# A two-layer encoder trunk: half of each row normalized from the sum just made on chip, x loaded two steps ahead, and the weight scalings moved into the output pass

## The chip, the cores and the metric

The kernel runs on one core of a Trainium2 chip. The metric is the device time of one execution in microseconds (us), the smaller the better. A change of 0.2% is about 5.5 us here.

## The reference

A sequence of 2048 rows of width 1024 goes through two layers. Cut to what matters:

```python
# layer A: gated MLP with a spatial mix in groups of 128 rows
h = rms_norm(x, a_norm_g)
u, v, z = split(h @ w_in, 3)                 # each 2048 x 2048
v = layer_norm(gelu(v), ln_g, ln_b)
y = gelu(u) * (w_s @ v + b_s) * silu(z)      # w_s masked by chunks of 64, per head
x = x + y @ w_out                            # 2048 x 2048 times 2048 x 1024
# layer B: attention over a band of 9 chunks of 64 rows
k, v = split(rms_norm(x, kv_norm_g) @ w_kv, 2)
q, z = split(rms_norm(x, b_norm_g) @ w_qz, 2)
o = softmax(q k^T / 8 + rel_bias) v
x = x + (o * silu(z)) @ w_out_b
return rms_norm(x, final_norm_g)
```

All is in float32. The kernel makes a float32 product out of three TensorE matmuls (high by high, high by low, low by high), after a split of each operand: ScalarE (ACT) casts the high half, VectorE (DVE) subtracts it for the low half.

## The kernel before, in words

**Products.** Layer A and the V projection are computed with Strassen's scheme in Winograd's form: a product of 2x2 block matrices in seven block products. The seven are called phases and are run in the order `PH = (1, 2, 6, 5, 7, 4, 3)`. In each phase an index j runs over 0 to 7, a pair of row blocks of 128 rows: block 2j is the upper half of the matrix (r = 0), block 2j+1 the lower (r = 1). One phase and one j make a step. A step of the passes in front (named n = 0 to 5: n = 0, 1 make v, n = 2 to 5 make u and z together, in quarters) has 12 matmuls of 512 columns, a step of the output pass ("o", y @ w_out) has 24, a step of the V pass ("v", x1 @ w_v) has 12. Tiles are P for n = 0 to 5, Po and Pv for the last two.

**Which phase finishes what.** A result block (r, c), c the half of the columns, is finished in phase 2 for (0,0), phase 7 for (1,1), phase 4 for (1,0) and phase 3 for (0,1); `evict` (L349) then adds the PSUM tile to a running sum in SBUF and calls `done_out` (L833) for the output pass. There x is added to it and the sum, x1 = x + y @ w_out, is stored to DRAM as `x1d`. So a row block 2j+1 is complete in step (phase 4, j), and 2j in step (phase 3, j).

**Order of the work.** `run_steps` emits, step by step, first the events of the step, then the matmuls, then the split of the left operand for three steps later (`LOOK = 3`), then the loads and splits of weights. `later(k, f)` puts f some steps on. The framework schedules from this, and each engine runs its own list strictly in order; so does SP, whose queue issues all DMAs: an issue that waits for a sum or a free buffer holds all issues behind it.

**Output pass, left operand.** Phase by phase, `prep_out` (L804) loads y blocks into tiles A (`y_load`, 4 buffers) and splits them into So. `s2_of` (L797) makes `sc` from three of them in steps 0 to 7. In phase 3 `prep_out` loads one block more and subtracts `sc` from it on VectorE (L822), three steps ahead of the product.

**Adding x.** For (0,0), (1,1) and (1,0) `done_out` loads x into a tile xr in the very step of the product (L851) and adds it one step later (L843): on VectorE for r = 0, on GpSimd (POOL) for r = 1. For (0,1), `x_ahead` (L854) loads x in phase 4 and adds it to the running sum on GpSimd (L857) before phase 3 has been added.

**Rows for V.** When the four pieces are in DRAM, `row_load` (L928) loads a block's two halves back into tiles bx, at the steps nin+43+j (odd blocks) and nin+51+j (even blocks), nin being the first step of the output pass; it has 56 steps, so most even blocks come in the V pass. Two steps on, `row_norm` (L936) squares both halves on ScalarE (jn, L941), adds the two sums on VectorE (L945, tile rn), raises to -1/2 on GpSimd (L946), and scales both halves on ScalarE (bx, L950). Four steps on, `row_flip` (L954) has TensorE transpose the eight 128x128 tiles into tn (L960), ScalarE copies them (L962), and they are stored as `xTd` for the V pass and the layer behind it. A transpose stands in TensorE's list between the matmuls of two steps, so what it waits for, those matmuls wait for too.

**Scalings.** Eleven weight blocks (eight of w_v, three of the first K, Q, Z projection) are multiplied by the norm gains on GpSimd and stored back (`scaled`, L878: a load of 512 KB into a `raw` tile, a multiply two steps on, a store four steps on). Before them come eight jobs (`o_sums`, `o_last`) that make the combinations of w_out. All nineteen sit at the places of the list `spare` (L913), before the start of phases 5, 7, 4, 3 of n = 2 and 1, 5, 7, 4, 3 of n = 3, 4, 5. The four `raw` buffers are shared with the loads of every pass's weights (rw, rwo, rwv). Sums and x tiles share the 25 buffers of the tag `acc`.

Of the kernel before, what the change touches and what calls it, by code (L numbers as in the profile page):

```python
# [12 lines left out]
AF = mybir.ActivationFunctionType  # L13
ALU = mybir.AluOpType
# [3 lines left out]
P = 128  # L18
# [9 lines left out]
EPS = 1e-6  # L28
# [5 lines left out]
def trunk_kernel(  # L34
# [19 lines left out]
    nc = tc.nc  # L54
# [4 lines left out]
    x1d = [dram.tile([T, D], F32, name=f"x1d{t}") for t in range(NT)]  # L59
# [24 lines left out]
    mhalf = cst.tile([P, 1], F32, name="mhalf")  # L84
# [116 lines left out]
    with ExitStack() as actx:  # L201
# [144 lines left out]
        xa = {}  # L346
        ya = {}
# [56 lines left out]
        def later(steps, f_):  # L404
            late.append((now[0] + steps, f_))
# [262 lines left out]
        start = {}  # L668
# [5 lines left out]
        def at(s, f_):  # L674
            events.setdefault(s, []).append(f_)

        for n in range(6):
            for ph in PH:
# [4 lines left out]
                elif n > 2:  # L683
                    o = -13 if ph == 6 else -5
# [103 lines left out]
        sc = {}  # L788

        def y_load(r, c, j, ph):  # L790
            t = pos[0].tile([P, 2, 512], F32, tag="A", name=f"A{ph}_{r}{c}_{j}", bufs=4)
            nc.sync.dma_start(t[:], ytd[r, c, j][:])
            return t[:]

        tv, tg = nc.vector.tensor_tensor, nc.gpsimd.tensor_tensor

        def s2_of(j):  # L797
# [3 lines left out]
                pieces(a[:, g], a[:, g], b[:, g], add)  # L801
            tv(sc[j], a, sc[j], op=sub)

        def prep_out(ph, j):  # L804
            if ph == 1:
                v = sc[j] = pos[0].tile([P, 2, 512], F32, tag="sc", name=f"sc{j}", bufs=8)[:]
                nc.sync.dma_start(v, ytd[0, 0, j][:])
            elif ph == 2:
                v = y_load(0, 1, j, ph)
            elif ph == 6:  # L810
                v = sc[j]
            elif ph == 5:
                v, b = y_load(1, 0, j, ph), y_load(1, 1, j, ph)
                tv(v, v, b, op=add)
            elif ph == 7:
                v, b = y_load(0, 0, j, ph), y_load(1, 0, j, ph)
                tv(v, v, b, op=sub)
            elif ph == 4:
                v = y_load(1, 1, j, ph)
            else:  # L820
                v, a = sc[j], y_load(0, 1, j, ph)
                tv(v, a, v, op=sub)  # L822
            views = []
            for g in range(2):
                t = s_tile(f"So{ph}_{j}_{g}")
                split(
                    t[:, 0].rearrange("p a b -> p (a b)"),
                    t[:, 1].rearrange("p a b -> p (a b)"), v[:, g, :], "So",
                )
                views += s_views(t)  # L830
            return views

        def done_out(n, r, c, j, t):  # L833
            blk = 2 * j + r
            cs = slice(c * 512, c * 512 + 512)
            rs = slice(blk % TB * P, (blk % TB + 1) * P)

            def store():
                nc.sync.dma_start(x1d[blk // TB][rs, cs], t)

            if (r, c) != (0, 1):
                xr = x_rows(r, c, j)
                later(1, lambda: (tg if r else tv)(t, t, xr, op=add))  # L843
                later(2, store)
            else:
                later(1, store)

        def x_rows(r, c, j):
            blk = 2 * j + r
            xr = acc_tile(f"xr{blk}_{c}")  # L850
            nc.sync.dma_start(xr[:], x[blk * P : (blk + 1) * P, c * 512 : c * 512 + 512])  # L851
            return xr[:]

        def x_ahead(r, c, j):  # L854
            xr = x_rows(r, c, j)
            s_ = (xa if r else ya)["o", j][:]
            later(2, lambda: tg(s_, s_, xr, op=add))  # L857

        def act_out(s, ph, j, views):
            flush(s)  # L860
# [4 lines left out]
        nin = start["o", 1]  # L865
# [8 lines left out]
            add_t(ts, start["o", ph], "o", ph, rows_o, 4, where, None, offs)  # L874
        for j in range(NJ):
            at(nin + j, lambda j=j: s2_of(j))
            at(start["o", 4] + j + 1, lambda j=j: x_ahead(0, 1, j))
        def scaled(src, name, gain, keep):  # L878
            raw = sh.tile([P, 1024], F32, tag="raw", name=f"raw_{name}", bufs=4)
            nc.sync.dma_start(raw[:], src)  # L880
            k = gain.shape[1]
            r3 = raw[:].rearrange("p (k c) -> p k c", k=k)
            later(2, lambda: nc.gpsimd.tensor_tensor(
                r3, r3, gain.broadcast_to([P, k, 1024 // k]), op=mul
            ))
            later(4, lambda: nc.sync.dma_start(keep, raw[:]))

        jobs = [
            (w_vv[r, c, q], f"bv{r}{c}{q}", kg[:, 4 * r + 2 * q : 4 * r + 2 * q + 2, :],
# [20 lines left out]
            later(2, lambda: tg(a, a, c[:], op=sub))  # L910
            later(4, lambda: nc.sync.dma_start(wos[4, q][:], a))

        spare = [(n, ph) for n in (2, 3, 4, 5) for ph in (1, 5, 7, 4, 3)][1:]  # L913
        todo = [lambda q=q, f_=f_: f_(q) for q in range(4) for f_ in (o_sums, o_last)]
        todo += [lambda job=job: scaled(*job) for job in jobs]
        for at_, f_ in zip(spare, todo):
            at(start[at_] - 3, f_)

        nxp = []
        xn = {}  # L920
# [6 lines left out]

        def row_load(blk):  # L928
            t, b = divmod(blk, TB)
            xn[blk] = [acc_tile(f"bx{blk}_{c}") for c in range(2)]  # L930
            for c, xt in enumerate(xn[blk]):
                nc.sync.dma_start(
                    xt[:], x1d[t][b * P : (b + 1) * P, c * 512 : c * 512 + 512]
                )

        def row_norm(blk):  # L936
            xs = xn[blk]
            jk = nxp[0].tile([P, 2, 512], BF16, tag="xv", name=f"jn{blk}", bufs=4)
            rs = [sm.tile([P, 1], F32, tag="rr", name=f"rn{blk}_{c}", bufs=6) for c in range(2)]
            for c in range(2):  # L940
                nc.scalar.activation(  # L941
                    jk[:, c, :], xs[c][:], AF.Square, scale=1.0 / 32, accum_out=rs[c][:],
                )
            r = rs[0]
            nc.vector.tensor_scalar(r[:], r[:], rs[1][:], EPS, op0=add, op1=add)  # L945
            nc.gpsimd.tensor_tensor(r[:], r[:], mhalf[:], op=ALU.pow)  # L946

            def scale():
                for xt in xs:
                    nc.scalar.mul(xt[:], xt[:], r[:])  # L950

            later(2, scale)

# [91 lines left out]
        for ph in PH:  # L1045
            if ph == 1:
                where, offs = in_big("v", ph, ("hh",)), ((-5, 1), (-4, 1), (-3, 1))
            else:
                where = in_t("v", ph)
                o = -12 if ph == 6 else -6  # L1050
# [3 lines left out]
                chain_in("v", "hl"), offs,  # L1054
            )
        for j in range(NJ):
            for blk, s_ in ((2 * j + 1, nin + 43 + j), (2 * j, nin + 51 + j)):
                ts.setdefault(s_, []).append(lambda blk=blk: row_load(blk))
                at(s_ + 2, lambda blk=blk: row_norm(blk))
                at(s_ + 4, lambda blk=blk: row_flip(blk))  # L1060
            at(nv + 2 + 9 * j // 8, lambda j=j: s7_of_v(j))
            at(start["v", 6] + 2 + j, lambda j=j: s4_of_v(j))
# [474 lines left out]
```

## Time and profile before

| what | value |
|---|---|
| three runs | 2740.37, 2740.96, 2745.56 us; median 2740.96 |
| the profiled execution | 2740.26 us |
| its span, first to last instruction | 2738.5 us |
| TensorE (PE) busy | 2648.9 us, 97% |
| VectorE, ScalarE, GpSimd busy | 1964.3, 1317.9, 781.7 us |
| granted TensorE clock, mean | 0.989 |
| output pass, first to last matmul, about | 1067 to 1387 us |
| V pass, about | 1388 to 1560 us |

The profile counts an engine as busy while an instruction of its own runs; matmuls overlap, so the time that TensorE loses is read from its waits and from the rows of equal windows. In a row of the waits stand the waiting engine, the tile and line, what it waited for, and the total, the count and the longest in us. In a row of windows stand the window, its length, the busy time of PE, the weight loads, DVE, ACT and POOL with their counts, the granted clock, the share of the DMA engines and GB/s. In a row of the timeline stand the start, the duration, the engine (SPq is SP's DMA queue), line, operation, out<-in, and in brackets the idle time before it and what ended that. Groups end in: busy us, mean ns of one | idle before, and its releasers.

### The profile page before, as it was taken

To read this page: it belongs to the slowest core of one execution; us is meant where nothing else is said; L and a number is where in the kernel's file an instruction comes from. 1 tells how busy PE (TensorE), PEld (TensorE's weight loads), DVE (VectorE), ACT (ScalarE), POOL (GpSimd) and SP (SyncE) were. 2 spreads that over 40 slices of the span, in tenths; PEclk is the share of its full clock that TensorE was granted. 3 is DMA by queue.
4 is the path that set the end of the run, shared out by engine and by line. 5 is a ranking of instruction groups with operands and counts; after the bars stand their busy time and mean duration, and the time that the engine had idled before them with its cause. 6 is when DMAs were issued, how large, how long until landed. Compare 5 with 4: busy or idle time off the path is not lost. (4 is left out here: it accounts for less than half of the span.)

```text
span 2738.5 us, 38612 instructions
## 1 busy us (share of the span) xinstructions
PE 2648.9 (97%) x13312; PEld 2208.3 (81%) x13312; DVE 1964.3 (72%) x3089; ACT 1317.9 (48%) x2290; POOL 781.7 (29%) x759
## 2 busy tenths in 40 slices
PE   9999999999899999999798999999999999999997
PEld 7888888778788888888676777878888888888886
DVE  5765667576667677667447867778878888878887
ACT  6422243433433434323472555655666566746663
POOL 4512036234142333002325544302221222212221
PEclk9999999999999999999999999999999999999999
DMA  8899999988999988757897687555556545555431
GB/s 307 307 347 336 315 336 334 332 323 316 329 320 324 334 320 290 252 176 251 255 323 231 231 287 242 182 163 175 159 169 195 157 148 153 184 167 162 137 124 62
DMA packets 268835, 667.91 MB, mean 244 GB/s; under 512 B 26592, under 2 KB 71648, under 8 KB 268640
## 3 DMA queue, kind: packets, MB, share of 16 engines
q1 hardware_dynamic: 268640, 665.44, 71.8%
q8 instruction: 106, 1.74, 0.3%
q14 instruction: 89, 0.73, 0.1%
HBM read 505.95 MB, written 148.90 MB: 239 GB/s over the span
## 5 line engine op out<-in xcount | busy, mean ns | idle before, releaser
L103 PE MATMUL P<-T,S 128*128 128x512 f32 x1248 | 498.8, 400 | 18.7 <-DMA S<-hsd 16.9
L105 PE MATMUL P<-T,S 128*128 128x512 f32 x1248 | 490.3, 393 | 0.0
L104 PE MATMUL P<-T,S 128*128 128x512 f32 x1248 | 489.6, 392 | 0.6 <-DVE T L250 0.6
L1228 POOL TENSOR_SCALAR pr<-pr,sl 128x640 f32<-128x640 f32 (+4 forms) x256 | 209.0, 817 | 714.1 <-DVE sl L1227 661.9
L103 PE MATMUL pj<-hh_b,wh_b 128*128 128x512 f32 x768 | 314.3, 409 | 2.5 <-ACT hh_b L139 2.5
L104 PE MATMUL pj<-hl_b,wh_b 128*128 128x512 f32 x768 | 304.3, 396 | 1.2 <-DVE hl_b L140 1.1
L105 PE MATMUL pj<-hh_b,wl_b 128*128 128x512 f32 x768 | 302.9, 394 | 0.0
L103 PEld LDWEIGHTS P<-T,S 128*128 128x128 f32 x1248 | 236.2, 189 | 66.2 <-issue 17.3
L105 PEld LDWEIGHTS P<-T,S 128*128 128x128 f32 x1248 | 236.1, 189 | 51.3
L104 PEld LDWEIGHTS P<-T,S 128*128 128x128 f32 x1248 | 236.5, 190 | 45.0 <-DVE T L250 1.0
L1224 ACT ACTIVATE pr<-pr,nm 128x640 f32<-128x640 f32 (+4 forms) x256 | 195.6, 764 | 120.1 <-DVE nm L1217 115.0
L1252 DVE TENSOR_TENSOR pt<-tp,pt 128x640 fp32r<-128x640 f32 (+4 forms) x256 | 188.5, 736 | 56.6 <-ACT pt L1251 54.8
L1251 ACT CAST pt<-tp 128x640 fp32r<-128x640 f32 (+4 forms) x256 | 159.1, 622 | 133.5 <-PE tp L1248 130.5
L1217 DVE CUSTOM_DVE_ANT_0 pr<-s,bias 128x640 f32<-128x640 f32 (+4 forms) x256 | 188.1, 735 | 27.4 <-PE s L1209 23.1
L1248 PEld LDWEIGHTS tp<-ident,pr 128*128 128x128 f32 x1120 | 131.9, 141 | 50.9 <-issue 14.9
L1248 PE MATMUL tp<-ident,pr 128*128 128x128 f32 x1120 | 166.3, 274 | 5.7 <-POOL pr L1228 2.9
L105 PEld LDWEIGHTS pj<-hh_b,wl_b 128*128 128x128 f32 x768 | 145.0, 189 | 29.6
L103 PEld LDWEIGHTS pj<-hh_b,wh_b 128*128 128x128 f32 x768 | 145.2, 189 | 20.6 <-ACT hh_b L139 3.9
L104 PEld LDWEIGHTS pj<-hl_b,wh_b 128*128 128x128 f32 x768 | 145.6, 190 | 16.3 <-DVE hl_b L140 2.5
L178 DVE TENSOR_TENSOR wl_b<-raw_b,wh_b 128x1024 fp32r<-128x1024 f32 x96 | 124.7, 1299 | 25.0 <-ACT wh_b L177 23.3
L1275 PE MATMUL pv<-pt,V 128*128 128x256 f32 x960 | 139.5, 284 | 0.0
L177 ACT CAST wh_b<-raw_b 128x1024 fp32r<-128x1024 f32 x96 | 100.5, 1049 | 65.8 <-PE pj L104 36.7
(246 smaller groups left out, 5881.4 us busy)
## 6 DMA issues: line engine op xcount, KB each, us to landing
S<-hsd SPq DMA_DIRECT2D x288, 512.0 KB, 5.5
rw<-in_w_a SPq DMA_DIRECT2D x108, 512.0 KB, 5.8
raw_b<-wk SPq DMA_DIRECT2D x75, 512.0 KB, 4.0
A<-ytd SPq DMA_DIRECT2D x72, 512.0 KB, 4.9
hsd<-S SPq DMA_DIRECT2D x56, 512.0 KB, 4.5
V<-vhd SPq DMA_DIRECT2D x112, 256.0 KB, 4.6
bias<-reld SPq DMA_DIRECT2D x64, 320.0 KB, 3.0
raw_bo<-in_wb_out SPq DMA_DIRECT2D x36, 512.0 KB, 4.2
```

Of the source, the lines that this page charges most:

```text
L103: mm(ps, lh, rh, start=first, stop=False)
L104: mm(ps, lh, rl, start=False, stop=False)
L105: mm(ps, ll, rh, start=False, stop=last)
L177: nc.scalar.copy(wh[:], raw[:])
L178: nc.vector.tensor_tensor(wl[:], raw[:], wh[:].bitcast(F32), op=ALU.subtract)
L1217: nc.vector.tensor_tensor_reduce(out=pr[:, c0:].rearrange("p (a b) -> p a b", a=nseg), in0=ps[:, :nseg, :w], in1=bias[:, c0:].rearrange("p ...
L1224: nc.scalar.activation(pr[:, c0:], pr[:, c0:], AF.Exp, scale=-1.0, bias=nm[:], accum_out=sl[:])
L1228: nc.gpsimd.tensor_scalar(pr[:, c0:], pr[:, c0:], sl[:], 1.0, op0=ALU.mult, op1=ALU.mult)
L1248: tpose(tp[:, b, :], pr[:, b * P : (b + 1) * P], ident[:])
L1251: nc.scalar.copy(oh, tp[:, b0:5, :])
L1252: nc.vector.tensor_tensor(pt[:, 1, b0 + qq : 5 + qq, cs], tp[:, b0:5, :], oh.bitcast(F32), op=ALU.subtract)
L1275: mm(po[:, 0, :], keys(i), pt[:, j, i, :], start=(t == 0 and j == 0 and i == blocks[0]), stop=(j == 1 and i == blocks[-1]),)
```

## The change

1. `row_load` loads only one half of a block (c = 1 for odd blocks, c = 0 for even ones). The other half is the tile in which `done_out` has just summed it; it is kept for this (`halves_of`). The loads, norms and transposes of all blocks come three steps earlier: at nin+40+j and nin+48+j.
2. x for all four pieces is loaded at one step ahead of the product and added two steps after the load, one step after the product (`x_rows` from the events, `xin`). VectorE adds it for (0,0), (1,0), (0,1), GpSimd only for (1,1). `x_ahead` is gone.
3. The subtraction from `sc` for phase 3 (`s3_of`) is taken out of `prep_out`: its load and its subtraction, now on GpSimd, come in phase 4, five steps ahead of the split that needs it.
4. The eleven scalings move to the output pass, one in every fourth step (nin+2, nin+6, ... nin+42), and store three steps on. The eight jobs on w_out remain in the passes in front, at eight places instead of the first eight of nineteen: n = 3 before phases 1, 7, 3, n = 4 before 5, 4, n = 5 before 1, 7, 3.
5. In `row_norm` the addition of the sums and the power wait for the next step's `later`.

```diff
+        def s3_of(j):
+            a = y_load(0, 1, j, 3)
+            later(2, lambda: tg(sc[j], a, sc[j], op=sub))
...
             else:
-                v, a = sc[j], y_load(0, 1, j, ph)
-                tv(v, a, v, op=sub)
+                v = sc[j]
...
-            if (r, c) != (0, 1):
-                xr = x_rows(r, c, j)
-                later(1, lambda: (tg if r else tv)(t, t, xr, op=add))
-                later(2, store)
-            else:
-                later(1, store)
+            xr = xin.pop((r, c, j))
+            later(1, lambda: (tg if r == c == 1 else tv)(t, t, xr, op=add))
+            later(2, store)
+            if r != c:
+                halves_of[blk] = {c: t}
...
-        def x_ahead(r, c, j):
-            xr = x_rows(r, c, j)
-            s_ = (xa if r else ya)["o", j][:]
-            later(2, lambda: tg(s_, s_, xr, op=add))
+            xin[r, c, j] = xr[:]
...
-            at(start["o", 4] + j + 1, lambda j=j: x_ahead(0, 1, j))
+            at(start["o", 4] + j - 1, lambda j=j: s3_of(j))
+            for ph, r, c in ((2, 0, 0), (7, 1, 1), (4, 1, 0), (3, 0, 1)):
+                at(start["o", ph] + j - 1, lambda r=r, c=c, j=j: x_rows(r, c, j))
...
-            later(4, lambda: nc.sync.dma_start(keep, raw[:]))
+            later(3, lambda: nc.sync.dma_start(keep, raw[:]))
...
-        spare = [(n, ph) for n in (2, 3, 4, 5) for ph in (1, 5, 7, 4, 3)][1:]
+        spare = [(n, ph) for n in (3, 4, 5) for ph in (1, 5, 7, 4, 3)][::2]
...
-        todo += [lambda job=job: scaled(*job) for job in jobs]
...
+        for i, job in enumerate(jobs):
+            at(nin + 2 + 4 * i, lambda job=job: scaled(*job))
...
-            xn[blk] = [acc_tile(f"bx{blk}_{c}") for c in range(2)]
-            for c, xt in enumerate(xn[blk]):
-                nc.sync.dma_start(
-                    xt[:], x1d[t][b * P : (b + 1) * P, c * 512 : c * 512 + 512]
-                )
+            c = blk % 2
+            xt = acc_tile(f"bx{blk}_{c}")
+            nc.sync.dma_start(xt[:], x1d[t][b * P : (b + 1) * P, c * 512 : c * 512 + 512])
+            halves_of[blk][c] = xt[:]
...
-            for blk, s_ in ((2 * j + 1, nin + 43 + j), (2 * j, nin + 51 + j)):
+            for blk, s_ in ((2 * j + 1, start["o", 4] + j), (2 * j, start["o", 3] + j)):
```

What this does to the lists shows at two places. The first is VectorE's list in the output pass at the change from phase 4 to phase 3, before: `xo<-Po` is the eviction of a phase 4 step, `So` a split, `sc<-A` the subtraction for phase 3, `rn` the sum for the third row block.

```order
L351 TENSOR_TENSOR xo_9658<-Po_5_11294,xo_9658 128x512
L250 TENSOR_TENSOR So_0_1_11328<-sc_9272,So_0_1_11328 128x512
L822 TENSOR_TENSOR sc_9340<-A_01_2_11443,sc_9340 128x1024
L250 TENSOR_TENSOR So_1_0_11380<-sc_9306,So_1_0_11380 128x512
L351 TENSOR_TENSOR xo_9700<-Po_6_11349,xo_9700 128x512
L250 TENSOR_TENSOR So_1_1_11383<-sc_9306,So_1_1_11383 128x512
L822 TENSOR_TENSOR sc_9395<-A_01_3_11508,sc_9395 128x1024
L945 TENSOR_SCALAR rn_0_11404<-rn_0_11404,rn_1_11405 128x1
```

Here four subtractions, each with a load of its own, stand ahead of the third block's sum. In the changed kernel they stand in GpSimd's list, in phase 4, among the powers `rn` of the first blocks:

```order
L806 TENSOR_TENSOR sc_9351<-A_01_3_11145,sc_9351 128x1024
L885 TENSOR_TENSOR raw_b_0_2_11149<-raw_b_0_2_11149,bg 128x1024
L949 TENSOR_TENSOR rn_0_11152<-rn_0_11152,mhalf 128x1
L949 TENSOR_TENSOR rn_0_11208<-rn_0_11208,mhalf 128x1
L806 TENSOR_TENSOR sc_9405<-A_01_4_11203,sc_9405 128x1024
L806 TENSOR_TENSOR sc_9463<-A_01_5_11260,sc_9463 128x1024
L949 TENSOR_TENSOR rn_0_11276<-rn_0_11276,mhalf 128x1
L806 TENSOR_TENSOR sc_9518<-A_01_6_11328,sc_9518 128x1024
L949 TENSOR_TENSOR rn_0_11344<-rn_0_11344,mhalf 128x1
```

The subtraction has moved from ahead of a block's sum to ahead of a block's power. The second place is SP's list in phase 4, before:

```order
L932 DMA bx_0_11229<-x1d_60 128x512
L839 DMA x1d_60<-xo_9447 128x512
L932 DMA bx_1_11230<-x1d_60 128x512
L851 DMA xr_1_11233<-in_x 128x512
L851 DMA xr_0_11264<-in_x 128x512
L792 DMA A_11_7_11266<-ytd_1_7_317 128x1024
L932 DMA bx_0_11278<-x1d_60 128x512
L839 DMA x1d_61<-xo_9503 128x512
```

and in the changed kernel, where `A_01` is the block for the subtraction and `wk` the store of the last scaling:

```order
L842 DMA x1d_60<-xo_9403 128x512
L792 DMA A_11_6_11246<-ytd_1_6_316 128x1024
L935 DMA bx_1_11258<-x1d_61 128x512
L792 DMA A_01_5_11260<-ytd_1_5_299 128x1024
L856 DMA xr_0_11262<-in_x 128x512
L888 DMA wk_0_64<-raw_b_0_2_11149 128x1024
L842 DMA x1d_61<-xo_9461 128x512
L792 DMA A_11_7_11314<-ytd_1_7_317 128x1024
```

A round has one read of x instead of two and one read-back instead of two; the x that a store rests on was issued a round earlier, and the read-back no longer follows the store of the same column half by a round or two.

More of the change, by code (lines that the diff above doesn't have):

```diff
@@ L834, in done_out @@
             blk = 2 * j + r
-            cs = slice(c * 512, c * 512 + 512)
             rs = slice(blk % TB * P, (blk % TB + 1) * P)
             def store():
+                cs = slice(c * 512, c * 512 + 512)
                 nc.sync.dma_start(x1d[blk // TB][rs, cs], t)
-            if (r, c) != (0, 1):
-                xr = x_rows(r, c, j)
-                later(1, lambda: (tg if r else tv)(t, t, xr, op=add))
-                later(2, store)
-            else:
-                later(1, store)
+            xr = xin.pop((r, c, j))
[3 more added lines that the diff above has]
+                halves_of[blk] = {c: t}
+        xin = {}
+        halves_of = {}
         def x_rows(r, c, j):
@@ L851, in x_rows @@
             nc.sync.dma_start(xr[:], x[blk * P : (blk + 1) * P, c * 512 : c * 512 + 512])
-            return xr[:]
-        def x_ahead(r, c, j):
-            xr = x_rows(r, c, j)
-            s_ = (xa if r else ya)["o", j][:]
-            later(2, lambda: tg(s_, s_, xr, op=add))
+            xin[r, c, j] = xr[:]
         def act_out(s, ph, j, views):
@@ L929, in row_load @@
             t, b = divmod(blk, TB)
-            xn[blk] = [acc_tile(f"bx{blk}_{c}") for c in range(2)]
-            for c, xt in enumerate(xn[blk]):
-                nc.sync.dma_start(
-                    xt[:], x1d[t][b * P : (b + 1) * P, c * 512 : c * 512 + 512]
-                )
+            c = blk % 2
+            xt = acc_tile(f"bx{blk}_{c}")
+            nc.sync.dma_start(xt[:], x1d[t][b * P : (b + 1) * P, c * 512 : c * 512 + 512])
+            halves_of[blk][c] = xt[:]
         def row_norm(blk):
-            xs = xn[blk]
+            xs = xn[blk] = [halves_of[blk][c] for c in range(2)]
             jk = nxp[0].tile([P, 2, 512], BF16, tag="xv", name=f"jn{blk}", bufs=4)
@@ L941, in row_norm @@
                 nc.scalar.activation(
-                    jk[:, c, :], xs[c][:], AF.Square, scale=1.0 / 32, accum_out=rs[c][:],
+                    jk[:, c, :], xs[c], AF.Square, scale=1.0 / 32, accum_out=rs[c][:],
                 )
             r = rs[0]
-            nc.vector.tensor_scalar(r[:], r[:], rs[1][:], EPS, op0=add, op1=add)
-            nc.gpsimd.tensor_tensor(r[:], r[:], mhalf[:], op=ALU.pow)
+            later(1, lambda: (
+                nc.vector.tensor_scalar(r[:], r[:], rs[1][:], EPS, op0=add, op1=add),
+                nc.gpsimd.tensor_tensor(r[:], r[:], mhalf[:], op=ALU.pow),
+            ))
             def scale():
                 for xt in xs:
-                    nc.scalar.mul(xt[:], xt[:], r[:])
+                    nc.scalar.mul(xt, xt, r[:])
             later(2, scale)
```

## The prediction

> **What bounds the kernel now.** TensorE is busy nearly all the time, so the change can only win what TensorE waits. I read the page's span first, then TensorE's waits, then windows of 50 us around them, then the timeline of the longest.
>
> ```profile
> span 2738.5 us, 38612 instructions
> PE P L103 <- DMA S<-hsd: 16.9, 6, 6.2
> PE tn L960 <- ACT bx L950: 16.8, 5, 12.3
> PE Pv L103 <- DVE cv L351: 6.1, 5, 1.7
> PE Pv L103 <- DVE yv L351: 4.0, 1, 4.0
> PE Pv L103 <- ACT vo L1026: 2.8, 2, 1.7
> PE Po L103 <- ACT So L247: 2.6, 3, 1.1
> ```
>
> Three stages hold these waits: the passes in front (S, 16.9), the output pass (the one of 12.3 on tn, and So 2.6) and the V pass (the other four on tn, cv, yv, vo).
>
> ```profile
> 500.00:550.00 50.00, 44.24 (x208) 34.97 (x206) 27.71 (x30) 20.71 (x34) 13.56 (x7) 0.97 0.94 346
> 550.00:600.00 50.00, 46.29 (x211) 38.91 (x212) 38.21 (x43) 17.43 (x28) 16.91 (x10) 0.93 0.87 315
> 700.00:750.00 50.00, 43.09 (x200) 35.00 (x200) 29.02 (x34) 21.03 (x35) 11.44 (x6) 0.93 0.94 347
> 1150.00:1200.00 50.00, 50.00 (x222) 41.42 (x221) 32.64 (x43) 18.92 (x27) 0.00 (x0) 1.00 0.45 151
> 1300.00:1350.00 50.00, 34.53 (x153) 26.88 (x152) 18.80 (x24) 15.76 (x32) 20.16 (x16) 0.88 0.73 235
> 1400.00:1450.00 50.00, 42.43 (x195) 33.60 (x193) 35.05 (x42) 33.38 (x63) 18.70 (x11) 0.97 0.89 275
> 1450.00:1500.00 50.00, 43.37 (x182) 34.77 (x183) 39.74 (x45) 16.38 (x26) 32.39 (x18) 0.97 0.80 255
> 1500.00:1550.00 50.00, 47.13 (x206) 38.12 (x205) 40.09 (x51) 23.34 (x36) 19.09 (x11) 1.00 0.60 209
> ```
>
> Length less PE's busy time gives the idle: 5.8 + 3.7 + 6.9 = 16.4 us in front, 15.5 in the output pass, 7.6 + 6.6 + 2.9 = 17.1 in the V pass. The undisturbed window has 222 matmuls, 0.225 us each. The DMA share is 0.87 to 0.94 where the loads of S are late, 0.45 in the middle of the output pass. The longest wait, in the timeline:
>
> ```profile
> 1320.71 0.93 SPq L851 DMA_DIRECT2D xr<-in_x  x2
> 1326.10 1.29 POOL L857 TENSOR_TENSOR yo<-yo,xr 128x512 f32<-128x512 f32 x1 [4.76 <-DMA xr<-in_x]
> 1328.67 0.32 SPq L839 DMA_DIRECT2D x1d<-xo  x1
> 1330.00 0.90 SPq L851 DMA_DIRECT2D xr<-in_x  x2
> 1330.94 0.43 SPq L792 DMA_DIRECT2D A<-ytd  x1
> ...
> 1336.09 1.66 DVE L822 TENSOR_TENSOR sc<-A,sc 128x1024 f32<-128x1024 f32 x1 [4.57 <-DMA A<-ytd]
> ...
> 1344.83 1.23 DVE L822 TENSOR_TENSOR sc<-A,sc 128x1024 f32<-128x1024 f32 x1 [5.27 <-DMA A<-ytd]
> 1345.97 0.21 DVE L945 TENSOR_SCALAR rn<-rn,rn 128x1 f32<-128x1 f32 x1
> ...
> 1346.25 0.93 POOL L946 TENSOR_TENSOR rn<-rn,mhalf 128x1 f32<-128x1 f32 x1 [1.74 <-DVE rn L945]
> ...
> 1347.22 1.34 ACT L950 ACTIVATE bx<-bx,rn 128x512 f32<-128x512 f32 x2 [8.73 <-POOL rn L946]
> ...
> 1347.99 1.33 PE L960 MATMUL tn<-ident,bx 128*128 128x128 f32 x5 [12.31 <-ACT bx L950]
> ```
>
> It is a ring through SP. SP issues x; GpSimd waits for it; the store of x1d waits for GpSimd; the next x and the next A stand behind that store on SP. One turn takes 1330.00 − 1320.71 = 9.3 us. A block's sum rn stands behind VectorE's subtraction, and that waits for the A of the turn. TensorE's list has the transposes ahead of the next product, so it stands still.
>
> **The change part by part.**
>
> ```profile
> L247 ACT CAST So<-sc 128x512 fp32r<-128x512 f32 x48 | 29.5, 619 | 46.5 <-PE Po L105 33.1 <-DVE sc L822 9.8 <-PE P L105 3.7
> L950 ACT ACTIVATE bx<-bx,rn 128x512 f32<-128x512 f32 x32 | 21.9, 719 | 23.0 <-POOL rn L946 23.0
> L941 ACT ACTIVATE jn<-bx 128x512 bf16<-128x512 f32 x32 | 19.9, 627 | 14.4 <-DMA bx<-x1d 14.4
> L960 PE MATMUL tn<-ident,bx 128*128 128x128 f32 x128 | 18.8, 286 | 16.8 <-ACT bx L950 16.8
> L962 ACT COPY xo<-tn 128x1024 f32<-128x1024 f32 x16 | 16.2, 1010 | 0.3 <-PE tn L960 0.3
> L883 POOL TENSOR_TENSOR raw_bv<-raw_bv,kg 128x1024 f32<-128x1024 f32 x8 | 15.5, 1940 | 61.1 <-DMA raw_bv<-in_w_vv 33.9 <-issue 27.2
> L822 DVE TENSOR_TENSOR sc<-A,sc 128x1024 f32<-128x1024 f32 x8 | 11.7, 1458 | 16.3 <-DMA A<-ytd 16.3
> L901 POOL TENSOR_TENSOR raw_o<-raw_o,raw_o 128x1024 f32<-128x1024 f32 x4 | 9.6, 2397 | 33.6 <-DMA S<-hsd 18.7 <-DMA raw_o<-in_w_out 14.9
> ```
>
> A step of the output pass with a block's transposes takes TensorE 24 x 0.225 + 18.8 / 16 = 6.6 us, without them 5.4. ScalarE needs in it two splits, two squares, two scalings and a copy: 1.24 + 1.25 + 1.44 + 1.01 = 4.9 us. So a turn of 9.3 us falls behind TensorE, and ScalarE's own work does not.
>
> *x two steps ahead, added by VectorE, one half read back.* The ring is cut in three places: x is a turn older when it is added, the adder in phases 4 and 3 is no longer the engine that waits for other loads, and the half read back (phases 7 and 2) was stored steps ago. SP loses 16 read-backs of 32. VectorE gains 16 additions: each of the size of the 0.69 us row further below, one a step, hidden behind 6.6 us. What is late next there? The eviction itself, the square, the power: ScalarE at 4.9 of 6.6. The waits on tn and So in the window of 1300, 12.3 + 2.6 = 15 us, go; bounds 0 and 15.5. After such a wait TensorE's clock is below full (0.88 in that window); the slow matmuls behind it I count as nothing. **Gain 15.**
>
> *Blocks three steps earlier.* Twelve of sixteen blocks are now transposed inside the output pass instead of nine. In a V step TensorE has 12 x 0.225 + 1.2 = 3.9 us and ScalarE 0.62 for one split and 3.7 for a block, 4.3 and the copies of Pv besides, so there ScalarE is the slower. The four shorter waits on tn, 16.8 − 12.3 = 4.5 us, mostly go (3.5). The waits on cv, yv and vo, 12.9 us, come from VectorE and GpSimd in the pass itself; the rows arrive some 20 us sooner (three steps of 6.6), which helps the loads that start them, but the combinations of w_v on GpSimd stay. I take 5.5 of them, less than half. Bounds 0 and 17.1. **Gain 9.**
>
> *Fewer jobs in front.* Eleven scalings of a 512 KB load and a store leave, and the w_out jobs move up: n = 2 has none, n = 4 none before phase 1. The waits for S lie in the windows from 500 to 600 and from 700, in n = 3 and n = 4. Before phase 1 of n = 3 there was a job `o_sums` and there is one again, so I leave the 9.5 us there; of the 6.9 after 700 I take 5, as the place before it is empty now. Bounds 0 and 16.4. **Gain 5.**
>
> *Scalings in the output pass.*
>
> ```profile
> raw_bv<-in_w_vv SPq DMA_DIRECT2D x8, 512.0 KB, 5.8
> A<-ytd SPq DMA_DIRECT2D x72, 512.0 KB, 4.9
> ```
>
> Per job, SP may stand from load to store: 5.8 + 1.9 = 7.7 us when nothing stands between them, as the list has it once or twice. Behind it wait the loads of A and of w_out; ScalarE and VectorE wait for those, then TensorE. The cover is the look-ahead of three steps, 16.2 us. One job fits under it; without the cover eleven would cost up to 85. DMA has room (0.45). Bounds 0 and, where two fall together four times, 22 (worked below). GpSimd's eight subtractions of 2.4 us (the row of L901 is the same operation and size) and the 21 us of scalings are hidden where TensorE waits for nothing on GpSimd; the powers of phase 4 are the exception. I take **a cost of 4** for both, near the lower end, since neither row in the pass nor its DMA share shows a shortage.
>
> The sum: 15 + 9 + 5 − 4 = 25 us. The profiled execution took 2740.26 us, 1.8 more than its span and 0.7 less than the median of the runs, 2740.96. 2740.3 − 25 = **2715**.
>
> *A rule that speaks against it.* While GpSimd works, VectorE is slowed:
>
> ```profile
> 1422.27 0.69 DVE L1013 TENSOR_TENSOR s<-sv,As 128x512 f32<-128x512 f32 x1
> 1422.88 2.39 POOL L254 TENSOR_TENSOR chv<-rwv,rwv 128x1024 f32<-128x1024 f32 x1 [2.14 <-DMA rwv<-wvs]
> 1422.99 2.83 DVE L1014 TENSOR_TENSOR sv<-As,s 128x512 f32<-128x512 f32 x1
> ```
>
> The same kind of operation takes 2.83 us beside a GpSimd instruction and 0.69 before it: 2.1 more. The Trainium skill (SBUF — State Buffer, Who interferes with whom) says that a VectorE instruction with two inputs in SBUF and a GpSimd instruction that reads SBUF share a port, and that the second to start waits for the whole of the first. By that rule the trace agrees. What it would make of the time is a rival below.
>
> **The rivals.**
>
> *All three stages are cleared* and the scalings cost nothing: 15 + 17 + 16 = 48, 2692 us. For it: DMA falls in front and the blocks are early. Against it: `o_sums` stands before n = 3 again. 16%.
>
> *Only the ring goes*: the V pass has its waits from GpSimd's and VectorE's own order, and the S waits from the loads of phase 6. 15 − 4 = 11, 2729 us. For it: cv, yv and vo are not rows of the norm. 18%.
>
> *GpSimd holds VectorE.* Eight subtractions now fall beside the additions of x that the squares of phase 4 need; 8 x 2.1 = 17 us reach TensorE, if a block's two steps of slack are used up. 25 − 17 = 8, 2732 us. Against it: VectorE has about 33 of 50 us busy here. 6%.
>
> *Given back in SP.* Two scalings and an A fall together: 2 x 7.7 + 4.9 + 2 for the split = 22, less the cover 16 = 6, four times about 22. 25 − 22 = 3, 2737 us, no change. 9%.
>
> *Slower: the power behind the subtraction.* GpSimd's list in phase 4 has subtractions ahead of powers, each with a load of its own, as VectorE's had them ahead of the sums. If the ring only changes engine, the eight subtractions (8 x 2.4 = 19.2) and the 16.3 us that they waited for A stand on the path of the transposes: 35.5 lost against 15 won, and the rest of the gain is not seen because the blocks are late: 2740.3 + 20.5 = 2761 us. It decides when A's issue is later than its slack: from A to the transposes 4.9 + 2.4 + 0.9 + 1.3 = 9.5 us have two steps of 6.6, so from 3.7 us of lateness. For it: SP has two A loads a step in phase 4. Against it: the subtraction is due five steps before its split. 9%.
>
> **How the numbers follow.** My forecast has 42%: 2715, itself 2705 to 2724. Faster by over 0.2% (5.5 us, about what can be told from no change here): 42 + 16 + 18 + 6 = 82%. Within it, 9%; slower, 9%. The range takes in all but the slower case and what lies below full clearing: 2690 to 2738.
>
> **What would show it.** Right: no wait on tn of over 3 us in the output pass, SP's turns in phase 4 as long as TensorE's steps, no wait of GpSimd for x there; in the V pass the waits on tn gone, those on cv smaller; the window from 700 full, that from 500 as now. Wrong: waits of Po for So in phases 6 and 5 with SP standing at a store of `wvs`; waits of tn for bx with GpSimd at the subtraction, waiting for A; VectorE's additions of over 2 us in phase 4; or V-pass waits as long as now.

## The result and the profile after

The changed kernel takes 2699.45 us (median of four runs, 2698.34 to 2700.79), the kernel before beside it 2741.20 (2740.37 to 2745.56). The ratio is 0.9845, with a 95% interval of 0.9828 to 0.9862: faster by 41.75 us where 25 were forecast. The profiled execution took 2700.79 us, its span is 2699.0.

TensorE's waits in the changed kernel (total, count, longest):

```profile
PE tn L964 <- ACT bx L954: 10.5, 2, 10.0
PE s L1213 <- DMA Qh<-Qh: 7.3, 1, 7.3
PE Pv L103 <- DVE cv L351: 3.9, 2, 3.8
PE P L103 <- DMA S<-hsd: 3.3, 3, 1.7
PE tn L964 <- ACT yo L954: 1.9, 1, 1.9
PE tn L964 <- ACT xo L954: 1.5, 2, 1.2
```

The waits for S in the passes in front fell from 16.9 to 3.3 us, those on So, yv and vo are gone. But one long wait on tn is still there, 10.0 us. The same kernel's windows of 50 us tell where it is:

```profile
500.00:550.00 50.00, 48.01 (x236) 39.24 (x235) 30.91 (x37) 21.48 (x37) 14.61 (x7) 1.00 0.94 341
550.00:600.00 50.00, 50.00 (x246) 42.30 (x245) 38.65 (x47) 19.90 (x33) 19.70 (x11) 1.00 0.88 312
700.00:750.00 50.00, 50.00 (x246) 42.22 (x245) 32.20 (x35) 24.63 (x41) 17.85 (x9) 1.00 0.91 344
1300.00:1350.00 50.00, 49.72 (x251) 41.26 (x250) 25.25 (x44) 37.96 (x74) 4.41 (x8) 1.00 1.00 310
1350.00:1400.00 50.00, 38.10 (x173) 31.36 (x172) 25.67 (x34) 29.48 (x54) 13.13 (x9) 0.90 0.86 263
```

In front TensorE now stands 2.0 us in these windows where it stood 16.4, at full clock. The DMA share there has hardly moved (0.94, 0.88, 0.91 against 0.94, 0.87, 0.94), so that share does not tell whether S comes late. The output pass (the window of 1300) has its TensorE back. The hole is at 1350, in the V pass, which now runs from 1356 to 1534.

The ring through SP turns as fast as TensorE's steps. SP's list in phase 4 of the changed kernel, x loads and stores of x1:

```profile
1285.83 0.43 SPq L856 DMA_DIRECT2D xr<-in_x  x1
1288.47 0.32 SPq L842 DMA_DIRECT2D x1d<-xo  x1
...
1297.02 1.08 SPq L856 DMA_DIRECT2D xr<-in_x  x1
1301.05 0.32 SPq L842 DMA_DIRECT2D x1d<-xo  x1
...
1303.06 1.07 SPq L856 DMA_DIRECT2D xr<-in_x  x1
```

One turn was 9.3 us; now three turns take 1303.06 − 1285.83 = 17.2 us, 5.7 each (the load at 1291.38 is in the rows left out).

**Where the time went, by stage.** From the timelines: the passes n = 3 and 4 from one cast of `ws` (ScalarE, three steps before the pass) to the next, n = 5 to the first Po, the output pass from the first Po to the first Pv, the V pass to the first pj, the rest to the end of the span. The first column is what lies ahead of n = 3. All in us, one profiled execution each. By these marks the output pass of the kernel before runs from 1060.7 to 1394.9 us and its V pass to 1576.9; the figures in the table ahead of the prediction (1067 to 1387, 1388 to 1560) are off.

| kernel | to n = 3 | n = 3 | n = 4 | n = 5 | output | V | rest | span |
|---|---|---|---|---|---|---|---|---|
| before | 509.3 | 187.2 | 181.1 | 183.2 | 334.2 | 182.0 | 1161.6 | 2738.5 |
| changed | 510.2 | 172.0 | 172.5 | 180.3 | 321.2 | 177.5 | 1165.3 | 2699.0 |
| e1 scalings in front | 508.8 | 182.3 | 175.4 | 191.4 | 325.8 | 171.1 | 1160.3 | 2715.1 |
| e2 w_out jobs at old places | 510.4 | 186.5 | 174.6 | 180.2 | 322.1 | 175.1 | 1164.3 | 2713.3 |
| e10 before, jobs moved only | 511.6 | 172.0 | 173.0 | 180.4 | 337.0 | 182.9 | 1162.4 | 2719.3 |
| e11 before, x ahead only | 509.0 | 187.1 | 182.1 | 182.9 | 315.1 | 183.8 | 1162.1 | 2722.0 |
| e4 x as before | 512.4 | 174.1 | 170.4 | 180.1 | 334.3 | 176.0 | 1163.5 | 2710.8 |
| e12 x added on GpSimd | 510.3 | 173.0 | 170.6 | 180.6 | 322.4 | 176.1 | 1167.5 | 2700.4 |
| e7 rows late | 510.9 | 174.0 | 170.0 | 180.3 | 318.6 | 182.0 | 1161.3 | 2697.1 |
| e6 rows late, both halves | 511.3 | 174.6 | 171.6 | 180.4 | 324.1 | 184.6 | 1162.7 | 2709.4 |
| e5 w_v loads later | 513.5 | 173.6 | 171.8 | 180.6 | 323.0 | 173.7 | 1164.4 | 2700.5 |
| e8 powers first | 514.5 | 172.6 | 172.5 | 180.6 | 323.3 | 170.5 | 1160.0 | 2694.0 |
| e3 subtraction on VectorE | 509.8 | 175.9 | 172.0 | 180.6 | 317.7 | 169.4 | 1163.8 | 2689.2 |
| e9 both mends | 511.5 | 175.0 | 171.4 | 180.6 | 317.7 | 171.0 | 1161.7 | 2688.8 |

Changed against before: 25.6 us gained up to the first Po, 13.0 in the output pass, 4.5 in the V pass, 3.7 lost behind it.

How far one execution can be trusted shows where several kernels have the same code and jobs in a stage: ahead of n = 3 the changed kernel and e8 differ by 4.3 us, n = 3 goes from 172.0 to 175.9, the output pass of the changed kernel, e2, e5 and e8 from 321.2 to 323.3, the V pass of the changed kernel and e2 from 177.5 to 175.1. A difference of 2 or 3 us in one stage proves nothing by itself.

### The profile page after: what moved, and what is told of

Read it like the earlier page. It is cut to its first block, busy times and chain, and to the rows that moved or that the text cites. A ratio compares the mean times of both kernels' runs of the same rounds, so it can differ in the third digit from the quotient of the medians.

```text
span 2699.0 us, 38615 instructions
## 1 busy us (share of the span) xinstructions
PE 2636.6 (98%) x13312; PEld 2205.3 (82%) x13312; DVE 1977.7 (73%) x3097; ACT 1320.7 (49%) x2290; POOL 784.7 (29%) x751
## 4 chain that ended last, share of the span: by engine, by line
PE 37%; DVE 8%; DMA 3%; issue 2%; ACT 2%; POOL 1%; SPq 0%; DVEq 0%; POOLq 0%; ACTq 0%
PE pj L103 5%; PE pj L104 5%; PE pj L105 5%; PE s L1213 4%; PE tp L1252 4%; PE pv L1279 3%; PE bo L105 2%; PE bo L103 2%; PE bo L104 2%; PE Pv L105 1%; PE Pv L103 1%; PE Pv L104 1%; DVE pt L1256 1%; DMA raw_b<-in_w_kqz 1%; DVE pr L1221 1%
## 5 line engine op out<-in xcount | busy, mean ns | idle before, releaser
L1221 DVE CUSTOM_DVE_ANT_0 pr<-s,bias 128x640 f32<-128x640 f32 (+4 forms) x256 | 188.0, 734 | 32.1 <-PE s L1213 27.7
```

Of the source, the lines that this page charges most:

```text
L1221: nc.vector.tensor_tensor_reduce(out=pr[:, c0:].rearrange("p (a b) -> p a b", a=nseg), in0=ps[:, :nseg, :w], in1=bias[:, c0:].rearrange("p ...
```

## The experiments

The kernel before was timed beside each of three sets; its medians there were 2747.05 (e1, e2, e4, e5), 2746.25 (e8, e3, e7, e6) and 2745.72 us (e9 to e12). Ratios are to these, with 95% intervals; the changed kernel's is 0.9845, to the 2741.20 beside it. As the kernel before was some 5 us slower in these sets, a gap to the changed kernel is not the same by the times and by the ratios; both are given where it matters. Point 5 of the change was not run by itself. In the cuts of the edits, ... stands for lines left out.

**The front: which jobs, and where.** e1 puts the scalings back in front, at the places left free, with their stores four steps on as before; e2 puts the w_out jobs back at their old places; e10 is the kernel before with the jobs moved and nothing else.

```diff
 e1
-            later(3, lambda: nc.sync.dma_start(keep, raw[:]))
+            later(4, lambda: nc.sync.dma_start(keep, raw[:]))
...
-        for i, job in enumerate(jobs):
-            at(nin + 2 + 4 * i, lambda job=job: scaled(*job))
+        rest = [p_ for p_ in [(n, ph) for n in (2, 3, 4, 5) for ph in (1, 5, 7, 4, 3)][1:] if p_ not in spare]
+        for at_, job in zip(rest, jobs):
+            at(start[at_] - 3, lambda job=job: scaled(*job))
 e2
-        spare = [(n, ph) for n in (3, 4, 5) for ph in (1, 5, 7, 4, 3)][::2]
+        spare = [(n, ph) for n in (2, 3, 4, 5) for ph in (1, 5, 7, 4, 3)][1:]
```

> The changed kernel with the eleven scalings put back into the passes in front, at the eleven places of the old list that its eight w_out jobs leave free; all else as changed (2699.5 us). Theory A, crowding of the w_out jobs: in front it was the w_out jobs at every phase of n = 2 and 3 that held the raw buffers, and the scalings at n = 3 phase 3 and n = 4 phase 1 that did so around 700 us. Then the front keeps its gain in n = 3 and loses it again in n = 4 (7.4 us of idle time and 2 of slow matmuls), and the output pass wins back what the scalings cost there (forecast 4): 2699 + 9 - 4 = about 2704. Theory B, traffic: any nineteen jobs in front bring all the waits for S back: 2699 + 25 - 4 = about 2720. Theory C, the forecast's: the front is worth 5: about 2700.

> The changed kernel with the eight w_out jobs at their old places, the four phases after the second of n = 2 and the first four of n = 3; the scalings stay in the output pass. Theory A, crowding: the waits for S in n = 3 (8.9 us of idle time, 4.4 of slow matmuls) come back and those of n = 4 don't: 2699 + 13 = about 2712. Theory B, traffic: fewer jobs in front are enough, so nothing comes back: 2699, within 3.

> The kernel before with only the jobs moved as in the change: eleven scalings in the output pass, eight w_out jobs at eight thinner places. All of the rest as before, so the ring through SP is whole. Theory: the 25.6 us in front come from this part alone, and the scalings cost the output pass nothing: 2741 - 25 = 2716, ratio 0.991, with the wait of 12 us on tn still there. Rival: with the ring in place a scaling's load and store lengthen its turns, and the output pass loses 5 to 20: 2721 to 2736.

Measured: e1 2730.70 us (2716.95 to 2733.33; the profiled one is the shortest, by 11 us), ratio 0.993 (0.9904 to 0.9956). e2 2718.69, 0.9894 (0.9871 to 0.9918). e10 2720.34, 0.9911 (0.9887 to 0.9934).

e10 has the whole gain in front (first Po at 1037.1 us, before 1060.7) and gives back 2.8 in the output pass, where its longest wait on tn is 8.3 us. So the gain in front comes from the jobs alone. e2, 19 us slower than the changed kernel by the times and 13 by the ratios, loses 14.5 us in n = 3 and 2.1 in n = 4: crowding, as theory A has it. e1 loses in every pass, 10.3, 2.9 and 11.1, as theory B has it for nineteen jobs in front. These rows tell 16 us of a loss that is 31 by the times and 23 by the ratios, more than either theory gave; no trace shows where the rest lies. Neither theory fits both; what e1 and e2 have in common is that jobs stand at neighbouring phases. Taking the scalings out of the output pass gained nothing there (325.8 against 321.2). The V pass of e1 is 6.4 us shorter than the changed kernel's, and why stays open.

How a job makes S late shows in SP's list at the start of n = 3, in the kernel before (the row of ScalarE is the cast that marks the pass):

```profile
507.61 0.70 SPq L895 DMA_DIRECT2D raw_o<-in_w_out  x1
509.28 0.61 ACT L247 CAST ws<-wr 128x512 fp32r<-128x512 f32 x1
525.02 0.46 SPq L904 DMA_DIRECT2D wos<-raw_o  x1
...
530.50 3.42 SPq L275 DMA_DIRECT2D rw<-in_w_a  x4
541.40 5.36 SPq L275 DMA_DIRECT2D rw<-in_w_a  x4
547.28 1.95 SPq L383 DMA_DIRECT2D S<-hsd  x4
```

And in the changed kernel, with the same `o_sums` before the same phase:

```profile
510.21 0.62 ACT L247 CAST ws<-wr 128x512 fp32r<-128x512 f32 x1
519.05 0.38 SPq L906 DMA_DIRECT2D wos<-raw_o  x1
523.87 0.90 SPq L275 DMA_DIRECT2D rw<-in_w_a  x2
...
532.41 5.52 SPq L275 DMA_DIRECT2D rw<-in_w_a  x4
537.98 1.88 SPq L383 DMA_DIRECT2D S<-hsd  x4
```

The weights of phase 6 and the jobs share four `raw` buffers. Issuing four loads of rw takes 5.4 to 5.5 us, 3.7 and 3.8 of it a wait until GpSimd's combinations of the weights (`ch`, L254) have freed a buffer, and the loads of S stand behind. This is as long in both kernels; it comes at 541.40 − 509.28 = 32.1 us after the mark before and at 22.2 now. In the kernel before another job of w_out stands a phase earlier, `o_sums` loads its third tile as late as 507.61, and stores its last one at 525.02, 15.7 us after the mark; now it does at 8.8. With e2's old places it is the old picture:

```profile
510.44 0.61 ACT L247 CAST ws<-wr 128x512 fp32r<-128x512 f32 x1
526.03 0.54 SPq L906 DMA_DIRECT2D wos<-raw_o  x1
542.56 5.45 SPq L275 DMA_DIRECT2D rw<-in_w_a  x4
548.53 1.86 SPq L383 DMA_DIRECT2D S<-hsd  x4
```

15.6 and 32.1 us after the mark, though no scaling is in front. That the places of the w_out jobs make the difference in n = 3 is shown by e2; that it is their spacing, and that it acts through the buffers, is read from these lists.

**The ring: x alone, or not.** e11 is the kernel before with only x changed; e4 the changed kernel with x as before; e12 the changed kernel with x two steps ahead, but added by GpSimd in phases 4 and 3.

```diff
 e12
-            later(1, lambda: (tg if r == c == 1 else tv)(t, t, xr, op=add))
+            later(1, lambda: (tv if r == c == 0 else tg)(t, t, xr, op=add))
```

> The kernel before with only x changed: loaded two steps ahead and added by VectorE except for the quarter (1,1). Theory of the ring: x is what it turns on, so the waits on tn and So in the output pass go, 12 to 16 us: 2741 - 14 = 2727, ratio 0.995. Rival: with the subtraction on VectorE behind a load and both halves read back the turn stays longer than a step: under 5 us, ratio 0.998 to 1.

> The changed kernel with x as before: loaded in the step of the product and added one step later on VectorE for r = 0 and GpSimd for r = 1, and for the last quarter added ahead on GpSimd in phase 4. The rest is as changed: one half read back, subtraction on GpSimd in phase 4. Theory of the ring: x is the transfer that the ring turns on, so SP's turns in phase 4 grow to 9 us again, GpSimd waits for x, and TensorE waits for tn by over 5 us in the output pass: 2699 + 10 to 15 = 2709 to 2714. Rival: reading back one half and moving the subtraction cut the ring already: 2699, up to 3 more.

> The changed kernel with x added by GpSimd in phases 4 and 3 as well, still loaded two steps ahead. Theory: the time of the load is what cuts the ring, and the engine matters little: 2699.5, up to 4 more. Rival: the additions stand behind the subtractions, the scalings and the powers in GpSimd's list, and each addition comes late for its square: waits on tn in the output pass, 2705 to 2715.

Measured: e11 2724.17 us, 0.9936 (0.9915 to 0.9958); e4 2711.37, 0.986 (0.9836 to 0.9885); e12 2700.75, 0.9842 (0.9825 to 0.9859). TensorE's waits in e4:

```profile
PE tn L971 <- ACT xo L961: 11.4, 2, 8.5
PE tn L971 <- ACT bx L961: 5.5, 2, 3.5
```

The edit on x is the whole of it: alone it makes the output pass 19.1 us shorter, taken away it makes it 13.1 longer, and the engine that adds does not matter. (The whole loss of e4 is 11.9 us by the times but 4 by the ratios, with an interval that overlaps the changed kernel's; the waits above are the firmer evidence.) One thing is not separated: the edit also moves the last quarter's x out of phase 4, where SP had two loads of x in a step, into phase 3, and no run has the earlier load without that. The form expected of e4 was not quite right: its stores of x1 come 6.6 us apart, not 9, and the waits fall on the scaling of the half kept on chip. e11 also shows what lay behind the ring. Its waits on tn, all of them in the V pass, and then its timeline:

```profile
PE tn L955 <- ACT bx L945: 9.8, 2, 9.6
```

```profile
1379.86 0.21 DVE L940 TENSOR_SCALAR rn<-rn,rn 128x1 f32<-128x1 f32 x1 [1.03 <-ACT jn L936]
1388.65 2.34 POOL L254 TENSOR_TENSOR chv<-rwv,rwv 128x1024 f32<-128x1024 f32 x1 [15.36 <-DMA rwv<-wvs]
1390.94 0.55 POOL L941 TENSOR_TENSOR rn<-rn,mhalf 128x1 f32<-128x1 f32 x1
```

With the ring cut, a row's sum is ready at 1380.1 and its power comes at 1390.94: it stands behind a combination of w_v, for which GpSimd waits. The changed kernel has the same.

**The V pass: the power behind the combination.** The timeline of the changed kernel around its wait of 10.0 us:

```profile
1362.88 3.66 SPq L275 DMA_DIRECT2D rwv<-wvs  x2
1365.80 0.21 DVE L948 TENSOR_SCALAR rn<-rn,rn 128x1 f32<-128x1 f32 x1
1369.12 0.21 DVE L948 TENSOR_SCALAR rn<-rn,rn 128x1 f32<-128x1 f32 x1 [1.72 <-ACT jn L943]
1371.80 2.34 POOL L254 TENSOR_TENSOR chv<-rwv,rwv 128x1024 f32<-128x1024 f32 x1 [14.78 <-DMA rwv<-wvs]
1374.09 0.55 POOL L949 TENSOR_TENSOR rn<-rn,mhalf 128x1 f32<-128x1 f32 x1
1374.68 0.72 ACT L954 ACTIVATE bx<-bx,rn 128x512 f32<-128x512 f32 x1 [5.66 <-POOL rn L949]
1375.45 0.90 PE L964 MATMUL tn<-ident,bx 128*128 128x128 f32 x3 [9.99 <-ACT bx L954]
```

A sum is ready at 1366.0, its power of 0.55 us begins at 1374.09, and the transposes right behind. e5 moves the loads for the combination three steps; e8 orders each combination of w_v behind the last power issued ahead of it.

```diff
 e5
-                o = -12 if ph == 6 else -6
+                o = -9 if ph == 6 else -6
 e8
-                pieces(o, x_, y_, op)
+                ins = pieces(o, x_, y_, op)
+                if n == "v":
+                    behind(ins, last["power"])
...
+                last["power"] = ins.ins.name
```

> The changed kernel with the loads and combinations of w_v for phase 6 of the V pass three steps later, so that they stand behind the last two powers in GpSimd's list. Theory of the power behind the combination: the 10.0 us for which TensorE waits for tn there come from a power that was ready at 1366 us and stood until 1374 us behind a combination that waited for its load. Then they go, with some 2 us of slow matmuls behind them: 2699 - 10 to 12 = about 2688. Rival: the loads are late in any case (SP and the raw buffers), and a wait of phase 6 for its T takes the place: 2699 - 4 or less gained, or a loss.

> The changed kernel with one order added on GpSimd: no combination of w_v for the V pass before the last power that stands ahead of it in the program; loads, steps and work are as changed. (The run that moved the loads three steps left a combination ahead of two powers in GpSimd's list, so it did not test this.) Theory of the power behind the combination: the wait of 10.0 us on tn in the V pass goes and some 2 us of slow matmuls with it: a V pass of 166 to 168 us where it has 177.5, and 2699.5 - 9 to 12 = 2688 to 2691. Rival: the power is only first in a queue of late things (the scaling waits for the store of x1d, the combination for its load and TensorE for the T of phase 6): gain under 4.

Measured: e5 2699.77 us, 0.9825 (0.9804 to 0.9846), no different; the longest wait on tn was 8.7. The framework's scheduler still put the combination ahead of the last two powers in GpSimd's list, so e5 says nothing of the theory. e8 2694.38 us, 0.9804 (0.979 to 0.9819): its interval lies wholly below the changed kernel's; the gain is 5.1 us by the times and 11 by the ratios. In e8 the long wait is gone:

```profile
PE Pv L103 <- DVE cv L353: 6.1, 3, 4.6
PE tn L969 <- ACT bx L959: 4.1, 3, 2.4
PE tn L969 <- ACT yo L959: 2.5, 3, 1.3
```

The V pass is 7.0 us shorter, not 10 to 12: smaller waits on tn and cv take part of the place. So the theory holds and its size was too large.

**The subtraction for phase 3.** e3 puts it back on VectorE, in the preparation of its step, and its load with it, from phase 4 to phase 3; e9 is e3 and e8 together.

```diff
 e3
-        def s3_of(j):
...
-                v = sc[j]
+                v, a = sc[j], y_load(0, 1, j, ph)
+                tv(v, a, v, op=sub)
...
-            at(start["o", 4] + j - 1, lambda j=j: s3_of(j))
```

> The changed kernel with the subtraction for phase 3 back in the preparation of the step, with its load, on VectorE, three steps ahead; the rest as changed. Forecast's theory: with x two steps ahead the ring through SP is cut, so A comes in time and the sums rn behind the subtraction don't wait: 2699.5, up to 3 more. Rival: the place of the subtraction mattered by itself, since in phase 4 VectorE now has the additions of x too: waits on tn or So of 5 to 12 us in the output pass come back, 2705 to 2711.

> The changed kernel with two mends together: the subtraction for phase 3 back on VectorE in the preparation of its step, and the powers ahead of the combinations of w_v on GpSimd. Apart they measured 0.9793 and 0.9804 of the kernel before, the changed kernel 0.9845. Theory of two causes: the subtraction on GpSimd costs the output pass 3.5 us and starts the V pass's rows late, the combination ahead of the last power costs 4.1 of wait and about 2 of slow matmuls that are left with the first mend: together 0.977, about 2685 where the kernel before has 2746. Rival, one cause: both mends take away the same wait on tn, and what is left is late for another reason: 0.979, no better than the first alone.

Measured: e3 2691.46 us (2688.52 to 2692.32), 0.9793 (0.9778 to 0.9808); e9 2689.68, 0.9802 (0.9783 to 0.982). Nothing expected of e3 was right: it is faster than the changed kernel, by 8.0 us in the times and 14 by the ratios, with an interval below it. The two mends do not add, so the rival of e9, one cause, stands. e3 gains 3.5 us in the output pass and 8.1 in the V pass. What the move did in the output pass shows in the splits of A from 1240 to 1356 us, 18 in each (busy us, mean ns): first the changed kernel, then e3.

```profile
L250 DVE TENSOR_TENSOR So<-A,So 128x512 fp32r<-128x512 f32 x18 | 24.0, 1340 | 4.9 <-ACT So L247 4.9
```

```profile
L250 DVE TENSOR_TENSOR So<-A,So 128x512 fp32r<-128x512 f32 x18 | 14.9, 835 | 6.8 <-ACT So L247 6.5 <-DMA x1d<-xo 0.3
```

The long ones of the changed kernel lie beside the subtraction:

```profile
1284.90 2.39 POOL L806 TENSOR_TENSOR sc<-A,sc 128x1024 f32<-128x1024 f32 x1 [3.81 <-DMA A<-ytd]
1285.10 2.75 DVE L250 TENSOR_TENSOR So<-A,So 128x512 fp32r<-128x512 f32 x1
1287.77 0.68 DVE L845 TENSOR_TENSOR xo<-xo,xr 128x512 f32<-128x512 f32 x1
...
1288.65 0.55 POOL L949 TENSOR_TENSOR rn<-rn,mhalf 128x1 f32<-128x1 f32 x1 [1.35 <-DVE rn L948]
...
1290.01 0.66 PE L964 MATMUL tn<-ident,xo 128*128 128x128 f32 x4 [1.18 <-ACT xo L954]
```

A split that takes 0.69 us alone began 0.2 us after the subtraction and ended 0.6 us after it, at 1287.85. The Trainium skill (SBUF — State Buffer, Who interferes with whom) says that of two such instructions the second to start waits for the first to end; these rows agree. The last three rows show how that reaches TensorE: the addition of x for a row begins only as the split ends, its sum and its power follow, and the transposes wait 1.18 us for the scaling. In the whole output pass TensorE waits 2.0 us on tn in the changed kernel, and the profile of e3 shows no wait of it there. The rest of the 3.5 us is of the size of the scatter. In the V pass e3's combination began at 1367.67, 11.7 us after the first Pv, where the changed kernel's began 15.6 after, and its wait on tn was 4.1 us in place of 10.0. Why its rows and loads come earlier there was not separated, nor was the place of the load from that of the subtraction.

**The rows for V.** e7 takes them three steps later, at the old steps; e6 also reads both halves back.

```diff
 e7
-            for blk, s_ in ((2 * j + 1, start["o", 4] + j), (2 * j, start["o", 3] + j)):
+            for blk, s_ in ((2 * j + 1, nin + 43 + j), (2 * j, nin + 51 + j)):
 e6, besides
-            c = blk % 2
+            for c in range(2):
...
```

> The changed kernel with the rows for V three steps later, at the old steps; still one half of each read back. Theory: earlier blocks are worth what the four small waits on tn were, 3 to 5 us: 2703 to 2705. Rival: in the changed kernel the even blocks meet the combinations on GpSimd whenever they come, so a longer wait on tn takes the place, 2706 or more; or the blocks fall behind the combination as one and nothing changes, 2699.5 within 3.

> The changed kernel with the rows for V three steps later and both halves read back, as in the kernel before. Against the run with the rows late alone it tells what the half kept on chip is worth by itself. Theory: 16 loads of 256 KB less on SP's queue and no scaling that waits for the store of the same tile cancel: the same as that run within 3. Rival of the forecast: the loads are one of the cuts in the ring, 3 to 8 us more than that run, in waits on tn in the output pass.

Measured: e7 2701.65 us, 0.9833 (0.9817 to 0.9848); e6 2709.67, 0.9858 (0.9842 to 0.9875). Earlier rows alone are worth nothing that can be told, as the second rival had it: the V pass is 4.5 us longer with three blocks more in it, the output pass 2.6 shorter. The half kept on chip is worth about 8 us (5.5 in the output pass, 2.6 in V), though the two intervals overlap a little. That is the rival's answer, not the theory's, in its size; of e6's waits in the output pass 2.3 us are on tn, and 2.6 are on So.

## Why the prediction was right or wrong

The sign and the range held, and so did the term of the output pass. The forecast itself, 2705 to 2724, did not: 2699.45 is 16 us below its 2715. By stage, in the profiled executions, the term in front was 20.6 too small, the output pass 2.0 too small, the V pass 4.5 too large, and a loss of 3.7 behind it was not seen. That the time fell in the range is in part luck: its lower end, 2690, rests on 16.4 us as the most that the front could give, the front gave 9.2 more, and the shortfall of the V pass hid it.

**Output pass, 15 gained less 4 of cost: right.** It gained 13.0 with three blocks more in it, which are 3 x 18.8 / 16 = 3.5 us of transposes. x two steps ahead is worth 19.1 by itself (e11); about 1 of the 4 more than my 15 is the slow matmuls behind the wait of 12.3 us, which I counted as nothing; the rest I can't place. The cost of 4 came out as 3.5 for the subtraction in this pass (e3); for the scalings e10 has 2.8, little above the scatter, and e1 speaks against any. The signs named for this pass came true: the longest wait on tn here is 1.2 us, SP's turn is 5.7, and GpSimd no longer waits for x, for which it waited 26.9 us from 1290 to 1350 before.

**Passes in front, 5 gained: the step that failed most.** It was 25.6, above even the bound of 16.4. First, I left the waits of n = 3 as they were, since `o_sums` stands before it again. The job did stand there; what mattered was the job a phase ahead of it (e2). Without that the loads of rw come 10 us sooner, and n = 3 wins 15.2 us. So the sign that I gave, the window from 500 as now, was wrong. n = 4, where scalings stood at every phase, wins 8.6 (of which e1 gives back 2.9); which job did it there was not looked into. Second, idle time is not all that a wait costs. In the kernel before, behind the wait of 6.2 us, the starts of the matmuls:

```profile
736.62 0.77 PE L103 MATMUL P<-T,S 128*128 128x512 f32 x1 [6.21 <-DMA S<-hsd]
...
738.04 0.63 PE L103 MATMUL P<-T,S 128*128 128x512 f32 x1
738.47 0.63 PE L104 MATMUL P<-T,S 128*128 128x512 f32 x1
...
743.25 0.39 PE L103 MATMUL P<-T,S 128*128 128x512 f32 x1
743.48 0.40 PE L104 MATMUL P<-T,S 128*128 128x512 f32 x1
```

They start 0.43 us apart at first, then 0.23. Behind the three longest waits for S there are 5, 10 and 8 such matmuls, 23 x 0.2 = 4.6 us. With the idle time, 16.4 − 2.0 = 14.4, that makes 19.0 of the 25.6. The other 6 or 7 lie in n = 5 (2.9), where no wait is long, and in gaps too short for the rows; I did not resolve them.

**V pass, 9 gained: wrong.** It gained 4.5, and 3.5 of that are the three blocks that moved out. The waits on yv and vo went, those on cv fell from 6.1 to 3.9 us, as hoped. But the step by which the four shorter waits on tn mostly go failed: one of 10.0 took their place. All waits in the pass were 17.4 us and are 15.8, which is the sign of being wrong that I had named, V-pass waits as long as now. Its mechanism is the one that I gave to the slower rival, a power behind a large operation that waits for a load, with another operation in another pass. I had written that the combinations of w_v stay on GpSimd, and had not asked what the earlier rows would meet there. With the order mended (e8) or the subtraction back (e3) the pass is 170.5 or 169.4 us, 11.5 to 12.6 shorter than before, 8 to 9 of it without the moved blocks: the gain was there to be had.

**The rivals.** "All three cleared", 2692, is nearest in time, but its V pass was not cleared. "GpSimd holds VectorE" happened, at some 3.5 us of the 17 that I gave it, but to the splits: the additions of x took 0.68 us throughout phase 4, and one began late behind a split. "Slower" did not: in phase 4 the powers waited for their sums, not for the subtraction. "Given back in SP" fell with e10; its working has a slip, since four times 6 us is 24, not 22, which would have made it 2739 us.

**Behind the V pass** 3.7 us were lost that no step spoke of, with the wait for Qh at 7.3 us where it was 4.3. The stage runs the same code in all kernels here and took 1160.0 to 1167.5 us in those built on the changed one, so this is not laid to the change.

## What to carry to other kernels

When jobs share buffers and an in-order DMA queue with the main stream, ask of each job what the one before it still holds when it starts; the DMA share told nothing here. When a stall is removed, go through the in-order list of every engine in the next stage for a small operation that stands behind a large one with a load of its own. A step moved to an idle engine can still slow the busy one beside it: here the change takes 0.9845 of the time before, and 0.9793 without its move of the subtraction.

## What the runs showed of the hardware

Behind a long wait of TensorE matmuls of 512 columns start 0.43 us apart in place of 0.23, for some 4 us after the wait of 6.2. The Trainium skill (TensorE: Matmul & The Clock Gate, What's actually happening) says that the clock falls to half after an idle window of about 3.4 us and returns after as long a busy one; these starts agree with it in the rate. Each of the three longest waits for S cost 1 to 2 us more than its length. The length of the wait does not set the number of slow starts: about 4 came behind the 12.3 us in the output pass before, 12 behind the 3.8 us on cv in the changed kernel's V pass. Nor do the traces show 3.4 us as a limit: in the kernel before a wait of 2.54 us in the V pass was followed by 6 slow starts, in e8 one of 2.40 us by none; there the measurement decides.
